# Attention pipeline: transposes directly behind the scores, both minima first, and the next pair's evictions put off behind the probabilities

## The chip, the cores and the metric

One NeuronCore of a Trainium2 chip runs the whole program. The metric is device time in microseconds (us), from launch to end, lower is better. The kernel's time before is the median of three runs, 2943.85 us (2941.52 to 2948.66).

## What is computed

Two layers of a backbone over 1024 latent tokens (a grid of 16 rows by 64 columns) with 256 context tokens, model width 1024. The first layer mixes tokens with Fourier transforms and long convolutions, the second with attention; each ends with a gated feed-forward network. The change touches the attention of the second layer alone. It has 16 heads of 64 channels. A query sees a window of 8 rows by 16 columns of latent keys, with a position bias, and all 256 context keys. Queries are taken in chunks of 16 columns, whose windows share 32 key columns:

```python
s_loc = jnp.einsum("bcqhd,bicjhd->bhcqij", q_r, k_b).astype(jnp.float32) * scale + bias[None]
s_loc = jnp.where(col_ok[:, :, None, :], s_loc, -jnp.inf)
s_ctx = jnp.einsum("bcqhd,bjhd->bhcqj", q_r, kc).astype(jnp.float32) * scale
s = jnp.concatenate([s_loc.reshape(B_, H, n_chunk, NA_QCOLS, n_loc), s_ctx], axis=-1)
p = jax.nn.softmax(s, axis=-1).astype(v.dtype)
...
o = (jnp.einsum("bhcqij,bicjhd->bcqhd", p_loc, v_b)
     + jnp.einsum("bhcqj,bjhd->bcqhd", p[..., n_loc:], vc))
...
y_lat = neighbourhood_attention(q, k, v, kc, vc, rpb).reshape(B_, L, D_MODEL) @ w_out
```

## The kernel before, in words

Numbers are carried as a high and a low half (`wh`, `wl` and the like), so a product is three matmuls; "splitting" a result means a ScalarE instruction that rounds it to the high half and then a VectorE instruction that subtracts that half for the low one.

The attention stage works on 64 items: 8 pairs of heads, times 2 halves of the rows (`hf`), times 4 chunks of columns (`c`). An item holds 128 queries of both heads. The steps of an item are:

- `attn_bias`: GpSimd (POOL) loads two bias tiles of 128 x 384.
- `attn_scores`: twelve matmuls write four PSUM banks of the pool `sc`: for each of the two heads a context score of 256 columns (`pctx`) and a local one of 384 (`loc`). VectorE takes the minimum of the (negated) context scores (L2050), then adds the bias and takes the minimum over both (L2051, a custom instruction and its accumulator read); ScalarE takes the exponentials of context (L2053) and local part (L2055). This runs head by head. Then ScalarE casts the context probabilities to float16 (L2060), POOL subtracts for the low half (L2061), and a transposing DMA on SyncE's (SP's) queue turns both (L2062).
- `attn_turn`: TensorE (PE) transposes the local probabilities of both heads into two banks of the pool `tr` (L2073), three transposes each. `attn_turned` splits them: two ScalarE copies (L2081) and two VectorE subtractions (L2082). From item 52 on, the context probabilities are transposed by PE too (four transposes), and the second head's three come later, in `attn_late`.
- `attn_values`: 30 matmuls multiply probabilities and values. They write into the unused columns of the `pctx` bank of a later item (`free`), so they come after that bank's first exponential. VectorE then divides by the sum (reciprocal L2107, norm L2108). The last score matmuls of the item behind use banks that this norm reads.
- `attn_send`, for every fourth item: four transposes into a `tr` bank (L2119), a split (L2121, L2122), a store by POOL's queue.

Beside an item, PE works on the preparation of the next pair, `attn_prep` (`lin`): keys, context keys and queries, in groups of 24 matmuls that fill a bank of the pool `pq` (for pair 0, which is prepared ahead of the loop, a bank of `sc`). Whatever ends a group is issued at that place: a split of keys (L300, L302), context keys (L1971, L1972) or queries (L1978, L1979), and the splits of value tiles, which DMA brings (`value`: L1955 on POOL, L1956 on ScalarE, L1957 on VectorE). A pair's preparation takes 24 portions, three for each of eight items; `fetch` issues it up to a target. For the items of the last pair `first_part(0)`, the first part of the output projection, takes its place; its weights `w_out2` come by POOL's queue.

In the loop (`attention`) PE, ScalarE, VectorE and POOL run in the order in which the code issues; only SP's order is set by the scheduler. One round issues: the bias of item k+3, the send of k-2, the late transposes of k-1, the scores of k+1 with their whole softmax, a third of the preparation, the transposes of k, a third, the values of k-1, the split of the transposes of k, a third.

Of the kernel before, what the change touches and what calls it, by code (L numbers as in the profile page):

```python
# [10 lines left out]
F32 = mybir.dt.float32  # L11
# [190 lines left out]
class Builder:  # L202
# [1705 lines left out]
    def attn_prep(self, pr, u):  # L1908
# [8 lines left out]
        def lin(wh, wl, pc, view=lambda x: x):  # L1917
            nonlocal step, acc
            yield None
            acc = self.SC() if pr == 0 else self.PQ()  # L1920
            for kb in range(KB):
                for w, part in ((wh, 0), (wh, 1), (wl, 0)):
                    self.mm(acc[:, :WID[pc]], w[:, kb * P:(kb + 1) * P], view(u.ap(part, kb, pc)),
                            kb == 0 and w is wh and part == 0, kb == KB - 1 and w is wl)
                step += 1
                for c in range(5):
                    if step == loads[c]:
                        load(c)
                    if step == turns[c]:
                        value(c)  # L1930
                yield WID[pc] / 1024

        def by_chunk(x):
            return x.rearrange("p (r h c) -> p h r c", r=8, h=4)

# [27 lines left out]
        for pc in (0, 1, 2):  # L1963
            if pc == 1:
                wq = self.halves_of("wq", pr)
            yield from lin(*wk, pc)
            w = WID[pc]
            if pc < 2:
                self.split(acc, *(t[:, pc * 512:pc * 512 + w] for t in (kh, kl)))
            else:  # L1970
                nc.scalar.mul(kc[:, :w], acc[:, :w], -1.0)  # L1971
                nc.vector.scalar_tensor_tensor(kc[:, w:], acc[:, :w], -1.0, kc[:, :w].bitcast(F32), op0=MUL, op1=SUB)  # L1972
        for pc in (0, 1):
            if pc == 1 and pr < 7:
                self.aw = self.halves_of("wk", pr + 1)
            yield from lin(*wq, pc, by_chunk)
            qh, ql = self.S2(F32R), self.S2(F32R)
            nc.scalar.mul(qh, acc, self.qinv)  # L1978
            nc.vector.scalar_tensor_tensor(ql, acc, self.qinv, qh.bitcast(F32), op0=MUL, op1=SUB)  # L1979
            qs[pc] = (qh, ql)  # L1980
# [3 lines left out]
    def attention(self, u, fill):  # L1984
        self.prep, self.osb, self.aw = {}, {}, None
        self.od = [[self.DR([P, LAT], F16) for _ in range(2)] for _ in range(8)]
        self.accumulators(pq=2, sc=4, tr=2)
# [14 lines left out]

        for k in range(2):
            piece(self.attn_bias, k)
        e = mybir.EngineType
        with self.tc.manual_schedule(engines={e.PE, e.Activation, e.DVE, e.Pool}):
            for k in range(-1, 65):
                piece(self.attn_bias, k + 3)
                piece(self.attn_send, k - 2)
                piece(self.attn_late, k - 1)  # L2010
                piece(self.attn_scores, k + 1)
                fetch((k * 3 + 8) * n / 24)
                piece(self.attn_turn, k)
                fetch((k * 3 + 9) * n / 24)
                free = state[k + 1]["free"] if k + 1 < 64 else self.SC()[:, 256:]
                if 0 <= k - 1 < 64:
                    self.attn_values(state[k - 1], *items[k - 1], free)
                piece(self.attn_turned, k)
                fetch((k * 3 + 10) * n / 24)
            piece(self.attn_send, 63)  # L2020
# [12 lines left out]
    def attn_scores(self, s, pr, hf, c):  # L2033
# [3 lines left out]
        bias = s["bias"]  # L2037
# [3 lines left out]
        for acc, keys, w in ((pctx, kc, 256), (loc, kw, 384)):  # L2041
            for x, y in ((0, 0), (0, 1), (1, 0)):
                for hd in (0, 1):
                    r = slice(hd * 64, hd * 64 + 64)
                    self.mm(acc[hd][:, :w], qc[x][r], keys[y][r], x == 0 and y == 0, x == 1)
        st = self.pt.tile([P, 16], F32, tag="st", name=self.nm("st"))
        cm, mx, s["rv"] = (st[:, 2 * i:2 * i + 2] for i in range(3))
        pc = self.T()
        for i in (0, 1):
            nc.vector.tensor_reduce(cm[:, i:i + 1], pctx[i][:, :256], axis=AX, op=MIN)  # L2050
            nc.vector.tensor_tensor_reduce(bias[i], loc[i][:, :384], bias[i], -1.0, cm[:, i:i + 1], ADD, MIN,  # L2051
                                           mx[:, i:i + 1])
            nc.scalar.activation(pc[:, i * 256:i * 256 + 256], pctx[i][:, :256], AF.Exp, bias=mx[:, i:i + 1],  # L2053
                                 scale=-1.0)
            nc.scalar.activation(bias[i], bias[i], AF.Exp, bias=mx[:, i:i + 1], scale=-1.0)  # L2055
        s["pts"], s["free"] = [None] * 3, pctx[0][:, 256:]
# [10 lines left out]
    def attn_turn(self, s, *item):  # L2067

        s["ps"] = []
        for k, src, n in s["ways"][:2]:  # L2070
# [3 lines left out]
            s["ps"].append((k, ps, n * P))  # L2074
        del s["ways"][:2]

    def attn_turned(self, s, *item):

        for k, ps, w in s["ps"]:
            t = s["pts"][k] = self.S2(F16, 1024)  # L2080
            self.nc.scalar.copy(t[:, :w], ps[:, :w])  # L2081
            self.nc.vector.tensor_tensor(t[:, 512:512 + w], ps[:, :w], t[:, :w], SUB)  # L2082

    def attn_late(self, s, *item):

        if s["ways"]:
            self.attn_turn(s)
            self.attn_turned(s)
# [53 lines left out]
    def run(self):  # L2142
# [391 lines left out]
```

## Time and profile before

| what | value |
|---|---|
| median of the runs | 2943.85 us |
| the profiled execution's own time | 2943.7 us |
| its span, first to last instruction | 2941.8 us |
| mean granted TensorE clock | 0.979 |
| busy share: TensorE, VectorE, ScalarE, GpSimd | 94%, 71%, 55%, 20% |
| first score matmul of the loop | at 1802.49 us |
| last score matmuls of the loop's last item begin | at 2230.35 us |

All profile lines come from this one execution, on core 0. In a line of the timeline stand the start in us, the duration, the engine, the source line, the operation, output <- inputs, shapes, how many alike, and in brackets the time the engine had sat idle and what ended that. In a line of the waits stand who waited, for whom, the total in us, how often, and the longest. Names such as `sc`, `tr`, `pq` are PSUM banks, `wh` and `wl` weights, `s`, `t`, `g`, `tk` tiles in SBUF, `st` the minima and sums. Ends of matmuls are modelled, so a row's duration is longer than the distance to the next matmul, and idle time of PE is seen too short.

### The profile page before, as it was taken

The page shows a single profiled execution, that of the slowest core. Times are in us where ns is not written, and L with a number is a line of the kernel's source. Part 1 is how long each engine was busy: PE and PEld are TensorE (multiplying, and loading weights), DVE is VectorE, ACT ScalarE, POOL GpSimd, SP SyncE. Part 2 cuts the span into 40 slices and gives each one's busy share as a digit, 9 for nine tenths or more (in the row PEclk, how much of TensorE's full clock was granted, in tenths as well). Part 3 has the DMA queues.
Part 4 walks back from the last instruction along what each step waited for, and adds up shares of the span by engine and source line. Part 5 has one row for each costly group of instructions (what it writes and reads, how often), then busy time and mean ns, then how long its engine had stood idle before and what let it go on. Part 6 is the DMA issues. An engine that isn't in the chain of part 4 may idle for free. (4 is left out here: it accounts for less than half of the span.)

```text
span 2941.8 us, 46325 instructions
## 1 busy us (share of the span) xinstructions
PE 2765.3 (94%) x16419; PEld 1689.4 (57%) x16419; DVE 2078.4 (71%) x3857; ACT 1622.9 (55%) x2857; POOL 602.8 (20%) x993
## 2 busy tenths in 40 slices
PE   6989999899989999999999998999989999999998
PEld 3766557888879544444556744565655444444555
DVE  4778777675557898886886765666665778765755
ACT  4674325454665676655564554566553467564543
POOL 1012013354121121122120112333332022112000
PEclk8999999999999999999999999999999999999999
DMA  7574435359595665557994996766655566424753
GB/s 257 188 270 171 150 116 172 112 177 330 219 357 181 212 219 199 195 197 271 336 311 133 339 351 196 155 150 145 163 159 170 202 238 238 162 94 173 238 191 125
DMA packets 322083, 607.60 MB, mean 207 GB/s; under 512 B 89910, under 2 KB 129528, under 8 KB 321850
## 3 DMA queue, kind: packets, MB, share of 16 engines
q1 hardware_dynamic: 252378, 384.38, 40.0%
q0 software_dynamic: 67168, 216.06, 21.0%
q10 hardware_dynamic: 2304, 4.20, 0.4%
q8 instruction: 129, 2.11, 0.3%
q14 instruction: 104, 0.85, 0.1%
HBM read 455.33 MB, written 135.53 MB: 201 GB/s over the span
## 5 line engine op out<-in xcount | busy, mean ns | idle before, releaser
L1462 PE MATMUL ps<-s,s 128*128 128x512 f16 x2244 | 506.3, 381 | 10.2 <-ACT g L1467 6.0
L1462 PEld LDWEIGHTS <-s 128*128 128x128 f16 x2640 | 257.9, 98 | 328.7 <-issue 22.0
L296 PE MATMUL ps<-s,wh 128*128 128x256 f32 (+3 forms) x1764 | 399.3, 330 | 11.5 <-ACT wh L300 5.4
L1231 ACT ACTIVATE s<-s,c 128x512 f16<-128x512 f32 (+1 forms) x324 | 234.3, 753 | 150.8 <-DMA s<-d 85.6
L1232 DVE SCALAR_TENSOR_TENSOR s<-s,c,s 128x512 f16<-128x512 f32 (+1 forms) x324 | 247.6, 793 | 89.0 <-ACT s L1231 88.7
L1679 PE MATMUL ps<-s 128*128 128x512 f16 (+2 forms) x1308 | 303.6, 378 | 2.0 <-DVE s L1232 2.0
L296 PE MATMUL ps<-s,wl 128*128 128x256 f32 (+3 forms) x882 | 263.4, 331 | 3.3 <-DMA wl<-d 2.0
L296 PE MATMUL pq<-s,wh 128*128 128x512 f16 (+1 forms) x908 | 252.1, 354 | 5.9 <-DMA wh<-d 4.0
L1679 PEld LDWEIGHTS <-s 128*128 128x128 f16 x1536 | 148.4, 98 | 179.0 <-issue 6.8
L296 PEld LDWEIGHTS <-wh 128*128 128x128 f16 x1664 | 153.6, 99 | 163.0 <-issue 33.7
L287 POOL DMA_DIRECT2D d<-s x201 | 109.1, 543 | 648.9 <-DVE s L1523 186.0
L348 ACT CAST mat<-cs 128x1024 fp32r<-128x1024 f16 (+2 forms) x120 | 111.3, 935 | 139.4 <-PE ps L296 52.6
L296 PEld LDWEIGHTS ps<-s,wh 128*128 128x128 f32 x1088 | 177.3, 192 | 18.1 <-ACT wh L300 5.7
L296 PE MATMUL ps<-s,mat 128*128 128x512 f32 x696 | 182.0, 408 | 3.5 <-DVE s L302 3.2
L1462 PE MATMUL ps<-s,wh 128*128 128x512 f16 x608 | 182.2, 379 | 1.7 <-DVE g L1476 1.3
L296 PE MATMUL sc<-s,s 128*128 128x65 f16 (+3 forms) x2688 | 154.7, 234 | 16.5 <-DVE s L2108 10.0
L296 PEld LDWEIGHTS <-s 128*128 128x128 f16 x2400 | 114.4, 98 | 79.9 <-issue 12.4
L296 PE MATMUL pq<-s,wl 128*128 128x512 f16 (+1 forms) x454 | 157.9, 354 | 0.0
L296 PEld LDWEIGHTS ps<-s,mat 128*128 128x128 f32 x696 | 134.5, 195 | 37.7 <-DVE s L302 4.0
L1264 ACT ACTIVATE t<-s 128x1024 bf16<-128x1024 f32 (+1 forms) x164 | 141.5, 864 | 14.9 <-DVE c L483 9.4
L2053 ACT ACTIVATE t<-sc,st 128x256 f32<-128x256 f32 x128 | 60.7, 474 | 144.3 <-DVE st L2051 138.5
L296 PEld LDWEIGHTS <-wl 128*128 128x128 f16 x832 | 82.0, 99 | 83.2 <-DMA wl<-d 3.8
(445 smaller groups left out, 5603.3 us busy)
## 6 DMA issues: line engine op xcount, KB each, us to landing
s<-d SPq DMA_DIRECT2D x294, 256.0 KB, 4.4
d<-s POOLq DMA_DIRECT2D x157, 256.0 KB, 3.6
s<-in_down SPq DMA_DIRECT2D x154, 256.0 KB, 4.9
s<-in_ada_w POOLq DMA_DIRECT2D x48, 512.0 KB, 4.9
s<-in_gate SPq DMA_DIRECT2D x46, 512.0 KB, 4.0
s<-in_up SPq DMA_DIRECT2D x46, 512.0 KB, 4.2
d<-g POOLq DMA_DIRECT2D x87, 256.0 KB, 3.3
d<-tk POOLq DMA_DIRECT2D x82, 256.0 KB, 4.3
```

The source lines that it names most:

```text
L287: self.last_ldr = self.nc.gpsimd.dma_start(out, in_).ins
L296: return self.nc.tensor.matmul(o, l, r, start=st, stop=sp).ins
L348: self.nc.scalar.copy(m, st)
L1231: nc.scalar.activation(hi, src, AF.Copy, scale=scale)
L1232: nc.vector.scalar_tensor_tensor(lo, src, scale, hi, op0=MUL, op1=SUB)
L1264: self.nc.scalar.activation(junk[:, :t.shape[1]], t, AF.Abs, scale=2.0 ** -15, accum_out=st[:, k:k + 1])
L1462: nc.tensor.matmul(ps, x[:, sl], y, start=first and j == 0 and x is wh and y is xh, stop=j == 3 and x is wl, skip_group_check=True)
L1679: m = nc.tensor.matmul(acc[j][:, c0:c1], x[:, sl], y[:, xs], start=first and k == 0, stop=last and k == 2, skip_group_check=True)
L2053: nc.scalar.activation(pc[:, i * 256:i * 256 + 256], pctx[i][:, :256], AF.Exp, bias=mx[:, i:i + 1], scale=-1.0)
```

## The change

It has five parts.

1. The round is issued anew: send of k-2, scores of k+1 (matmuls only), transposes of k directly behind them, then the softmax of k+1, half of the preparation, the values of k-1, the late transposes of k with their split, half of the preparation.
2. The softmax (now `attn_softmax`) takes both heads' minima of the context first, then both heads' minima with bias and the exponentials. The split of the transposes (`turned`) is woven in: its ScalarE copies ahead of the first exponential, its VectorE subtractions behind the second minimum with bias.
3. What a group of the preparation ends with (splits of keys, context keys, queries and values) is collected in `self.later` and issued at the next `flush`: one stands behind the softmax, one behind the late transposes. For pair 0 it is issued at once, as before.
4. Pair 0's preparation uses the pool `pq`, and the pools are set up in the order `sc`, `tr`, `pq`.
5. The weights `w_out2` of the first part of the output projection are loaded by SP's queue instead of POOL's.

```diff
-            acc = self.SC() if pr == 0 else self.PQ()
+            acc = self.PQ()
...
                     if step == turns[c]:
-                        value(c)
+                        later(lambda c=c: value(c))
...
+        def later(work):
+            if pr == 0:
+                work()
+            else:
+                self.later.append(work)
...
-        self.accumulators(pq=2, sc=4, tr=2)
+        self.accumulators(sc=4, tr=2, pq=2)
...
+        def flush():
+            while self.later:
+                self.later.pop(0)()
...
                 piece(self.attn_send, k - 2)
-                piece(self.attn_late, k - 1)
                 piece(self.attn_scores, k + 1)
-                fetch((k * 3 + 8) * n / 24)
                 piece(self.attn_turn, k)
-                fetch((k * 3 + 9) * n / 24)
+                piece(self.attn_softmax, k + 1)
+                flush()
+                fetch((k * 3 + 8.5) * n / 24)
                 free = state[k + 1]["free"] if k + 1 < 64 else self.SC()[:, 256:]
                 if 0 <= k - 1 < 64:
                     self.attn_values(state[k - 1], *items[k - 1], free)
-                piece(self.attn_turned, k)
+                piece(self.attn_late, k)
+                flush()
                 fetch((k * 3 + 10) * n / 24)
+            flush()
...
         for i in (0, 1):
             nc.vector.tensor_reduce(cm[:, i:i + 1], pctx[i][:, :256], axis=AX, op=MIN)
+        for i in (0, 1):
             nc.vector.tensor_tensor_reduce(bias[i], loc[i][:, :384], bias[i], -1.0, cm[:, i:i + 1], ADD, MIN,
                                            mx[:, i:i + 1])
+            if i == 0:
+                self.turned(0)
             nc.scalar.activation(pc[:, i * 256:i * 256 + 256], pctx[i][:, :256], AF.Exp, bias=mx[:, i:i + 1],
                                  scale=-1.0)
             nc.scalar.activation(bias[i], bias[i], AF.Exp, bias=mx[:, i:i + 1], scale=-1.0)
+        self.turned(1)
...
-    def attn_turned(self, s, *item):
-
-        for k, ps, w in s["ps"]:
-            t = s["pts"][k] = self.S2(F16, 1024)
-            self.nc.scalar.copy(t[:, :w], ps[:, :w])
-            self.nc.vector.tensor_tensor(t[:, 512:512 + w], ps[:, :w], t[:, :w], SUB)
+    def turned(self, part):
+
+        for pts, k, ps, w in self.turns:
+            if part == 0:
+                t = pts[k] = self.S2(F16, 1024)
+                self.nc.scalar.copy(t[:, :w], ps[:, :w])
+            else:
+                t = pts[k]
+                self.nc.vector.tensor_tensor(t[:, 512:512 + w], ps[:, :w], t[:, :w], SUB)
+        if part:
+            self.turns = []
...
-                    (self.ld if pc else self.ldr)(x[:, :768], self.halves[("w_out2", nb)][:, k * 1024:k * 1024 + 768])
+                    self.ld(x[:, :768], self.halves[("w_out2", nb)][:, k * 1024:k * 1024 + 768])
```

The change moves what each engine does in a row. On VectorE, one item (one whose number modulo 8 is 2) stood so before: minimum and minimum with bias by head, a key split of the preparation (L302), the reciprocal and norm of the values, the subtractions from the `tr` banks, a value split (L1957).

```order
L2050 TENSOR_REDUCE st_19672<-sc_19658 128x1
L2051 ISA g_19429,st_19672<-sc_19656,g_19429,st_19672 128x384
L2051 ISA st_19672 128x1
L2050 TENSOR_REDUCE st_19672<-sc_19659 128x1
L2051 ISA s_4132_19431,st_19672<-sc_19657,s_4132_19431,st_19672 128x384
L2051 ISA st_19672 128x1
L302 TENSOR_TENSOR s_4112_19314<-pq_19481,s_4111_19313 128x512
L2107 RECIPROCAL st_19449<-sc_19658 128x2
L2108 TENSOR_TENSOR s_4181_19713<-sc_19658,st_19449 128x128
L2082 TENSOR_TENSOR s_4182_19746<-tr_19696,s_4182_19746 128x384
L2082 TENSOR_TENSOR s_4183_19749<-tr_19700,s_4183_19749 128x384
L1957 SCALAR_TENSOR_TENSOR s_4184_19755<-t_19488,c_17518,s_4184_19755 128x512
```

The same item on VectorE now (L2072, L2074 are the minima, L2110 the subtractions, L1975 the value split, L2138 and L2139 reciprocal and norm):

```order
L2072 TENSOR_REDUCE st_19676<-sc_19654 128x1
L2072 TENSOR_REDUCE st_19676<-sc_19655 128x1
L2074 ISA g_19429,st_19676<-sc_19652,g_19429,st_19676 128x384
L2074 ISA st_19676 128x1
L2074 ISA s_4132_19431,st_19676<-sc_19653,s_4132_19431,st_19676 128x384
L2074 ISA st_19676 128x1
L2110 TENSOR_TENSOR s_4177_19681<-tr_19668,s_4177_19681 128x384
L2110 TENSOR_TENSOR s_4178_19683<-tr_19672,s_4178_19683 128x384
L1975 SCALAR_TENSOR_TENSOR s_4181_19697<-t_19418,c_17518,s_4181_19697 128x512
L2138 RECIPROCAL st_19457<-sc_19654 128x2
L2139 TENSOR_TENSOR s_4183_19711<-sc_19654,st_19457 128x128
```

The subtractions moved ahead of the norm, the value split from behind the norm to ahead of it, and the key split to behind it. On ScalarE the same item had, before, exponentials, the cast L2060, the key split L300, the copies L2081 and the value split:

```order
L2053 ACTIVATE t_19673<-sc_19658,st_19672 128x256
L2055 ACTIVATE g_19429<-g_19429,st_19672 128x384
L2053 ACTIVATE t_19673<-sc_19659,st_19672 128x256
L2055 ACTIVATE s_4132_19431<-s_4132_19431,st_19672 128x384
L2060 CAST s_4176_19682<-t_19673 128x512
L300 CAST s_4111_19313<-pq_19481 128x512
L2081 CAST s_4182_19746<-tr_19696 128x384
L2081 CAST s_4183_19749<-tr_19700 128x384
L1956 ACTIVATE s_4184_19755<-t_19488,c_17518 128x8x64
```

On ScalarE now (L2107 the copies, L2078 and L2080 the exponentials, L2086 the cast, L1974 the value split):

```order
L2107 CAST s_4177_19681<-tr_19668 128x384
L2107 CAST s_4178_19683<-tr_19672 128x384
L2078 ACTIVATE t_19677<-sc_19654,st_19676 128x256
L2080 ACTIVATE g_19429<-g_19429,st_19676 128x384
L2078 ACTIVATE t_19677<-sc_19655,st_19676 128x256
L2080 ACTIVATE s_4132_19431<-s_4132_19431,st_19676 128x384
L2086 CAST s_4179_19692<-t_19677 128x512
L1974 ACTIVATE s_4181_19697<-t_19418,c_17518 128x8x64
L300 CAST s_4109_19309<-pq_19485 128x512
```

The copies moved from behind the cast to ahead of the first exponential. On PE the transposes stood behind the first third of the preparation (`pq` rows):

```order
L296 LDWEIGHTS wh_19104
L296 MATMUL pq_19689<-s_3554_16624,wh_19104 128x256
L296 LDWEIGHTS wl_19105
L296 MATMUL pq_19689<-s_3554_16624,wl_19105 128x256
L2073 MATMUL tr_19696<-c_86,g_19328 128x128 x3
L2073 MATMUL tr_19700<-c_86,s_4117_19330 128x128 x3
L296 LDWEIGHTS wh_19104
L296 MATMUL pq_19689<-s_3568_16677,wh_19104 128x256
```

Now, in the same item, they stand directly behind the last score matmuls (`sc` rows, 128x384):

```order
L296 MATMUL sc_19652<-s_3965_18449,s_4090_19158 128x384
L296 MATMUL sc_19653<-s_3965_18449,s_4090_19158 128x384
L2098 MATMUL tr_19668<-c_86,g_19324 128x128 x3
L2098 MATMUL tr_19672<-c_86,s_4115_19326 128x128 x3
L296 LDWEIGHTS wh_19100
L296 MATMUL pq_19701<-s_3554_16624,wh_19100 128x256
```

So the transposes come six preparation matmuls earlier here, and the preparation of a round is cut in two instead of three.

More of the change, by code (lines that the diff above doesn't have):

```diff
@@ L1934, in by_chunk, with key, context_key, query @@
             return x.rearrange("p (r h c) -> p h r c", r=8, h=4)
+        def later(work):
[3 more added lines that the diff above has]
+                self.later.append(work)
+        def key(acc, cols):
+            self.split(acc, kh[:, cols], kl[:, cols])
+        def context_key(acc):
+            nc.scalar.mul(kc[:, :256], acc[:, :256], -1.0)
+            nc.vector.scalar_tensor_tensor(kc[:, 256:], acc[:, :256], -1.0, kc[:, :256].bitcast(F32), op0=MUL, op1=SUB)
+        def query(acc, pc):
+            qh, ql = qs[pc] = self.S2(F32R), self.S2(F32R)
+            nc.scalar.mul(qh, acc, self.qinv)
+            nc.vector.scalar_tensor_tensor(ql, acc, self.qinv, qh.bitcast(F32), op0=MUL, op1=SUB)
         def load(c):
@@ L1966, in attn_prep @@
             yield from lin(*wk, pc)
[L1967 to L1972, printed above, removed]
+            later((lambda acc=acc: context_key(acc)) if pc == 2 else
+                  (lambda acc=acc, pc=pc: key(acc, slice(pc * 512, pc * 512 + 512))))
         for pc in (0, 1):
@@ L1976, in attn_prep @@
             yield from lin(*wq, pc, by_chunk)
[L1977 to L1980, printed above, removed]
+            later(lambda acc=acc, pc=pc: query(acc, pc))
         self.prep[pr] = (qs, (kh, kl), (kc[:, :256], kc[:, 256:]), vt)
@@ L1984, in attention @@
     def attention(self, u, fill):
-        self.prep, self.osb, self.aw = {}, {}, None
+        self.prep, self.osb, self.aw, self.later, self.turns = {}, {}, None, [], []
         self.od = [[self.DR([P, LAT], F16) for _ in range(2)] for _ in range(8)]
-        self.accumulators(pq=2, sc=4, tr=2)
+        self.accumulators(sc=4, tr=2, pq=2)
         n = sum(x or 0 for x in self.attn_prep(0, u))
@@ L2036, in attn_scores @@
         qs, kk, kc, _ = self.prep[pr]
-        bias = s["bias"]
         loc, pctx = ([self.SC(), self.SC()] for _ in range(2))
@@ L2045, in attn_scores, with attn_softmax @@
                     self.mm(acc[hd][:, :w], qc[x][r], keys[y][r], x == 0 and y == 0, x == 1)
+        s["pctx"], s["loc"], s["free"] = pctx, loc, pctx[0][:, 256:]
+    def attn_softmax(self, s, pr, hf, c):
+        nc = self.nc
+        pctx, loc, bias = s["pctx"], s["loc"], s["bias"]
         st = self.pt.tile([P, 16], F32, tag="st", name=self.nm("st"))
@@ L2055, in attn_scores @@
             nc.scalar.activation(bias[i], bias[i], AF.Exp, bias=mx[:, i:i + 1], scale=-1.0)
-        s["pts"], s["free"] = [None] * 3, pctx[0][:, 256:]
+        self.turned(1)
+        s["pts"] = [None] * 3
         s["ways"] = [(1, bias[0], 3), (2, bias[1], 3)]
@@ L2067, in attn_turn @@
     def attn_turn(self, s, *item):
-        s["ps"] = []
         for k, src, n in s["ways"][:2]:
@@ L2073, in attn_turn @@
                 self.nc.tensor.transpose(ps[:, j * P:(j + 1) * P], src[:, j * P:(j + 1) * P], self.ident)
-            s["ps"].append((k, ps, n * P))
+            self.turns.append((s["pts"], k, ps, n * P))
         del s["ways"][:2]
-    def attn_turned(self, s, *item):
-        for k, ps, w in s["ps"]:
-            t = s["pts"][k] = self.S2(F16, 1024)
-            self.nc.scalar.copy(t[:, :w], ps[:, :w])
-            self.nc.vector.tensor_tensor(t[:, 512:512 + w], ps[:, :w], t[:, :w], SUB)
+    def turned(self, part):
[8 more added lines that the diff above has]
+            self.turns = []
     def attn_late(self, s, *item):
@@ L2087, in attn_late @@
             self.attn_turn(s)
-            self.attn_turned(s)
+        self.turned(0)
+        self.turned(1)
     def attn_values(self, s, pr, hf, c, o):
```

## The prediction

> **What bounds the kernel now.** I read the page first, then the windows, the waits and the timeline of the attention stage, the only stage whose compute order the change touches. TensorE (PE) is the bound: it is busy 94% of the span.
>
> ```profile
> PE 2765.3 (94%) x16419; PEld 1689.4 (57%) x16419; DVE 2078.4 (71%) x3857; ACT 1622.9 (55%) x2857; POOL 602.8 (20%) x993
> ```
>
> So a gain is a PE wait that goes. The windows (us, then busy time of each engine with its instructions, last but two the granted PE clock) split the stage into 51 steady items (one item is one pair of heads, one half, one chunk), ten late ones, and the end of the loop; three of its stretches ran at half clock.
>
> ```profile
> 1817.33:2156.64 339.31, 309.13 (x3269) 204.74 (x3269) 220.74 (x588) 205.49 (x435) 120.50 (x202) 0.99 0.66 151
> 2156.64:2230.35 73.71, 62.24 (x633) 41.28 (x632) 47.05 (x122) 35.98 (x77) 21.32 (x40) 0.93 0.47 154
> 2230.35:2245.48 15.13, 14.45 (x160) 9.31 (x160) 7.92 (x20) 5.31 (x11) 3.72 (x7) 1.00 0.36 114
> ...
> 1771.20:1781.40 10.20, 4.58 (x11) 1.68 (x12) 8.79 (x19) 5.09 (x9) 4.39 (x14) 0.50 1.04 401
> ...
> 2170.50:2177.30 6.80, 6.10 (x37) 4.55 (x38) 3.63 (x10) 2.99 (x7) 0.73 (x2) 0.50 0.15 52
> 2197.80:2201.20 3.40, 3.40 (x36) 2.04 (x35) 1.08 (x4) 0.00 (x0) 0.85 (x2) 0.50 0.90 293
> ```
>
> PE's waits in the steady items, then in the late ones:
>
> ```profile
> PE tr L2119 <- DVE s L2082: 15.1, 12, 1.7
> PE sc L296 <- DVE s L2108: 10.0, 13, 1.0
> PE sc L296 <- ACT t L2053: 4.2, 7, 0.8
> ```
>
> ```profile
> PE tr L2073 <- DVE s L2082: 5.9, 5, 2.7
> PE pq L296 <- DMA wh<-d: 4.0, 2, 2.3
> PE tr L2119 <- DVE s L2082: 1.1, 2, 0.9
> ```
>
> Three kinds: transposes wait until VectorE (DVE) has read their bank (L2082); the eighth score matmul waits for the norm L2108, which reads the bank it writes; and in the late items weights come late. The steady items repeat every eight (the preparation of the next pair fills eight items). One cycle, from score start to score start:
>
> ```profile
> 1916.43 0.39 PE L296 MATMUL sc<-s,s 64*128 64x256 f32 x2
> ...
> 1969.70 0.39 PE L296 MATMUL sc<-s,s 64*128 64x256 f32 x2
> ```
>
> That is 53.27 us, 6.37 times in the 339.31. The timeline shows one item with its send before it and the next item behind it (S, the start of the scores, is 1951.72):
>
> ```profile
> 1951.16 0.63 PE L2119 MATMUL tr<-c,s 128*128 128x128 f32 x4 [0.81 <-DVE s L2082]
> ...
> 1951.72 1.16 PE L296 MATMUL sc<-s,s 64*128 64x256 f32 x12
> ...
> 1951.82 0.59 ACT L2121 CAST tk<-tr 128x512 f16<-128x512 f32 x1 [1.08 <-PE tr L2119]
> ...
> 1953.05 0.41 DVE L2050 TENSOR_REDUCE st<-sc 128x1 f32<-128x256 f32 x1
> ...
> 1953.60 0.62 DVE L2051 CUSTOM_DVE_ANT_0 g<-sc,g,st 128x384 f32<-128x384 f32 x1
> ...
> 1954.26 0.47 ACT L2053 ACTIVATE t<-sc,st 128x256 f32<-128x256 f32 x1 [1.85 <-DVE st L2051]
> ...
> 1954.63 0.60 ACT L2055 ACTIVATE g<-g,st 128x384 f32<-128x384 f32 x1
> ...
> 1955.68 0.59 PE L296 MATMUL pq<-s,wh 128*128 128x512 f16 x2
> ...
> 1955.72 0.60 ACT L2055 ACTIVATE s<-s,st 128x384 f32<-128x384 f32 x1
> ...
> 1956.23 0.60 ACT L2060 CAST s<-t 128x512 f16<-128x512 f32 x1
> ...
> 1956.33 0.59 PE L296 MATMUL pq<-s,wh 128*128 128x512 f16 x2
> ...
> 1956.73 0.69 ACT L1978 ACTIVATE s<-pq,c 128x512 fp32r<-128x512 f32 x1
> ...
> 1957.07 0.62 PE L296 MATMUL sc<-s,s 64*128 64x256 f32 x6
> ...
> 1957.46 0.75 DVE L1979 SCALAR_TENSOR_TENSOR s<-pq,c,s 128x512 fp32r<-128x512 f32 x1 [2.14 <-ACT s L1978]
> ...
> 1958.32 0.29 DVE L2108 TENSOR_TENSOR s<-sc,st 128x128 f32<-128x128 f32 x1
> ...
> 1958.76 0.77 PE L296 MATMUL sc<-s,s 64*128 64x384 f32 x5 [0.89 <-DVE s L2108]
> ```
>
> See two things. First, PE's own work: three preparation matmuls take 0.65 (1955.68 to 1956.33), 0.2155 each. This item (1951.72 to 1957.07) has 12 such matmuls, no PE idle and 5.35 us, so scores, transposes and values are 5.35 - 12 x 0.2155 = 2.76. A cycle holds 108 preparation matmuls of 512 columns' worth and two sends of 0.56 (1951.72 - 1951.16): 8 x 2.76 + 108 x 0.2155 + 1.12 = 46.5 us. So 6.8 of 53.27 are lost; the waits named sum to only 29.3 / 6.37 = 4.6, because matmul ends are modelled. Second, the chain that ends at 1958.76: exponentials, the cast L2060, an eviction pair (L1978, L1979) that stands ahead of the norm, the norm, PE.
>
> **The change, part by part.**
>
> *Preparation of pair 0 in pq banks.* PE sat idle before it, for a copy of a bank; its first weight load had come long before, and the copy of the pq bank was long done:
>
> ```profile
> 1768.60 0.56 ACT L1893 COPY tk<-pq 128x512 f32<-128x512 f32 x1
> ...
> 1771.70 0.10 PEld L296 LDWEIGHTS <-wh 128*128 128x128 f16 x1 [3.15 <-DMA wh<-d]
> ...
> 1776.82 1.01 PE L296 MATMUL sc<-s,wh 128*128 128x512 f16 x2 [7.77 <-ACT t L1893]
> ...
> 1804.29 0.80 PE L296 MATMUL sc<-s,s 64*128 64x384 f32 x5 [1.00 <-DVE s L1979]
> ```
>
> Now the weights decide: 1776.82 - 1771.70 = 5.1 earlier. The 1.00 at item 0 (its fourth score bank was still being evicted) goes too. Of half clock: 11 matmuls took 4.58 in the window against 11 x 0.2155 = 2.37; with 7.77 - 5.1 = 2.7 idle left instead of 7.77 I take 0.9 back of 2.2 (bounds 0 and 2.2). Together -7.0, bounds -5 and -8.4. The Trainium skill ("TensorE: Matmul & The Clock Gate", Part 1: The HAM clock gate) says that the clock halves after at least one idle window of about 3.4 us and comes back after a busy one; by it 2.7 us of idle would not halve it, and this part would be -8.3. The trace speaks against it: the half clock from 2170.50 lies round the late items' longest wait, 2.7 us, and no wait there is longer.
>
> *Steady items.* Transposes directly behind the scores, the copies ahead of the exponentials and the subtractions ahead of the norm free the tr banks early: the 15.1 us go. What is late next is the norm, since it still stands behind the deferred eviction, and the copies now precede the exponentials. Worked from S: transposes at 1.16 (the scores' length), first copy 0.55 later (an estimate from the send: copy 0.66 behind four transposes, three here), two copies of 0.37 each (an estimate from their 0.485 busy, pitch as for exponentials), first exponential 2.45. Then 0.37 + 0.51 twice gives the cast at 4.24, the eviction's ScalarE half at 4.74 (0.50). Query halves: DVE 0.73 later (1956.73 to 1957.46), the norm 0.86 behind it, PE 0.44 behind that: S + 6.77. Value halves:
>
> ```profile
> 1921.78 0.72 ACT L1956 ACTIVATE s<-t,c 128x512 f16<-128x512 f32 x1
> ...
> 1921.96 1.15 POOL L2061 TENSOR_TENSOR s<-t,s 128x512 f16<-128x512 f32 x1 [4.15 <-ACT s L2060]
> ...
> 1922.54 1.12 DVE L1957 SCALAR_TENSOR_TENSOR s<-t,c,s 128x512 f16<-128x512 f32 x1 [2.17 <-ACT s L1956]
> ...
> 1924.91 0.74 DVE L1957 SCALAR_TENSOR_TENSOR s<-t,c,s 128x512 f16<-128x512 f32 x1
> ```
>
> Their DVE half starts 0.76 later, and is 1.12 long beside the POOL subtraction of the cast instead of 0.74; the order now always puts them right behind that cast. The norm is then 0.86 + 1.12 - 0.75 = 1.23 behind: PE at 4.74 + 0.76 + 1.23 + 0.44 = S + 7.2. In the items behind a send the first minimum starts at S + 1.33 (1953.05), the exponential 0.42 + 0.55 + 0.66 later, so all is 0.45 later.
>
> PE reaches the next item's eighth score matmul 0.40 after its own work (at 1958.76 - 0.89 the seventh had ended, 0.80 behind S; an end lags the next start by 0.4, an estimate from 0.59 for two at 0.2155). Own work is 5.35 with 12 preparation matmuls, 6.0 with 15, 5.4 with 24 of half width. By position in the cycle (item number modulo 8), own work, norm at PE, wait: 2 (behind a send): 5.4, 7.6, 1.8; 3: 6.0, 7.2, 0.8; 4: 5.35, 7.2, 1.4; 5 (query and a value split of half size, a query's chain and some 0.4 more, then a send, which needs the norm at 6.0): 7.2, 1.2; 7 (query): 6.0, 6.8, 0.4; 6 (behind a send, nothing deferred): 0.3 for the exponential, whose bank the values are written in; 0 and 1: nothing ahead of the norm, 0. Sum 5.9: the cycle is 52.4, and (52.4 - 53.27) x 6.37 = -5.5. A wait shifts its whole item, so it isn't handed on. Bounds: each of six waits 0.4 shorter (value splits at 0.74): -15 more, so -20; each 0.5 longer (copies or the deferral later than I set them): +19, so +14. I take the middle, since its chain is that of the rows.
>
> *Late items (score matrices of three transposes).* The third transposes stand behind the values, when their bank has long been subtracted: of 7.0 us I take 6.4. Weights of the output projection leave POOL's queue for SP's, which in these items has no transposing DMA left. On POOL they stood behind a send's store and what that waits for:
>
> ```profile
> 2193.43 0.55 POOL L287 DMA_DIRECT2D d<-tk x1 [3.93 <-DVE tk L2122]
> ```
>
> I take all of the 4.0. SP's later loads move with it; I cost that at nothing, covered by the matmuls behind the stage, 3 us if not. The two half clocks cost (6.10 + 3.40) / 2 = 4.75; with those waits gone I take half, 2.5. -12.9, bounds -9 and -17. *The end of the loop* (15.13): its last transposes, too, stand behind scores or values: -1, bounds 0 and -2.
>
> **The sum** is made against the profiled execution's 2943.7, which is the median of the runs, 2943.85, within 0.2: 2943.7 - 7.0 - 5.5 - 12.9 - 1.0 = **2917.3**.
>
> **Rivals.**
> *Waits halve.* If the copies squeeze in before the exponentials for nothing and the value splits escape POOL, 3.0 of the cycle's loss remain: 49.5, -24, 2899; with none left, 46.5 and 2880. For it: most named waits are on L2082, which goes. Against: the norm's chain above. Chance 0.18.
> *The ring eats it.* Copies ahead of the exponentials push every norm 0.2 to 0.4 later than I set: the cycle is 53.3 to 54.3, and only the head, the late and the last items gain, 2923 to 2929. Chance 0.16.
> *Slower.* Each of the six later by nearly 1 us: cast, deferred eviction, norm and PE become one ring without slack, as the eviction waits for ScalarE, which waits for the transposes, which wait for the last norm. From S + 8.1 for the norm at PE it decides: 5.7 more a cycle, 58.1, +31 against -21, 2954. For it: the row at 1958.76 is such a ring already. Against: items 0, 1 and 6 have nothing ahead of the norm. Chance 0.06.
> *Head and tail don't come* (weights stand as late on SP, the pq bank isn't free): -5.5 alone, 2938. Chance 0.07.
> *The clock never falls* in the head and the late items, since no PE idle is left that is long enough: 1.3 + 2.3 more, 2914, inside my forecast's span; chance 0.1, part of the forecast's. The clock gate of the Trainium skill's page would give that.
>
> **How the numbers follow.** My forecast, 2908 to 2925, has 0.53. About what a measurement can tell from no change is 0.3%, 8.8 us: faster lies below 2935. Faster 0.53 + 0.18 + 0.14 and a little of the rest: 0.86; within 0.3%: 0.08; slower: 0.06. The range takes in the forecast, the eaten ring and most of the halved waits: 2892 to 2939.
>
> **Right or wrong.** Right: a first preparation matmul near 1771.7; no wait of the send on the subtraction at position 1; norm waits of 0.4 to 1.8 in positions 2, 3, 4, 7; cycle 52.4; late items near 61. Wrong: a cycle under 50 or over 53.3, the first matmul still behind a copy, weights still waited for.

## The result and the profile after

The changed kernel takes 2921.72 us (median of 4 runs, 2916.52 to 2925.08), the kernel before 2945.62 (4 runs, 2941.52 to 2948.66). The ratio is 0.9918 with a 95% interval of 0.9895 to 0.9941: 24 us faster. The forecast was 2917.3, in a range of 2892 to 2939. The profiled execution took 2916.52, its span is 2914.8.

Its windows for the head, the steady items (2 to 52) and the late items (53 to 62), to be laid beside those of before:

```profile
1771.20:1781.40 10.20, 9.09 (x29) 3.57 (x30) 9.17 (x21) 5.68 (x10) 4.38 (x14) 0.67 1.04 406
1812.15:2139.96 327.81, 309.84 (x3269) 205.31 (x3268) 220.85 (x586) 201.26 (x434) 120.61 (x202) 1.00 0.66 158
2139.96:2199.16 59.20, 57.11 (x632) 39.59 (x632) 45.19 (x123) 35.71 (x76) 15.00 (x29) 1.00 0.53 177
```

The steady items went from 339.31 to 327.81, the late ones from 73.71 to 59.20, and there the clock is full now. In the head PE waits for its weights and no longer for a copy:

```profile
1772.31 1.04 PE L296 MATMUL pq<-s,wh 128*128 128x512 f16 x2 [3.00 <-DMA wh<-d]
```

One cycle of eight items, from score start to score start:

```profile
1908.60 0.62 PE L296 MATMUL sc<-s,s 64*128 64x256 f32 x6
...
1960.04 0.80 PE L296 MATMUL sc<-s,s 64*128 64x256 f32 x8
```

That is 51.44 us, where it was 53.27 and PE's own work is 46.5. PE's waits in the steady items, then in the late ones (L2139 is the norm, L2150 the send's transposes, L2078 the first exponentials):

```profile
PE sc L296 <- DVE s L2139: 12.8, 20, 0.9
PE tr L2150 <- DVE s L2139: 3.5, 6, 0.6
PE sc L296 <- ACT t L2078: 1.7, 7, 0.3
```

```profile
PE sc L296 <- ACT t L2078: 1.6, 4, 0.4
PE sc L296 <- DVE s L2139: 0.4, 1, 0.4
```

In these items no wait is left for a subtraction from a `tr` bank, nor for weights. All that is left in the steady items hangs on the norm or on an exponential. The timeline of the item at position 2 and the start of the next shows the chain that sets it:

```profile
1915.07 1.16 PE L296 MATMUL sc<-s,s 64*128 64x256 f32 x12
...
1916.40 0.74 DVE L2072 TENSOR_REDUCE st<-sc 128x1 f32<-128x256 f32 x2
...
1917.78 0.47 ACT L2078 ACTIVATE t<-sc,st 128x256 f32<-128x256 f32 x1 [0.17 <-DVE st L2074]
...
1919.52 0.61 ACT L2086 CAST s<-t 128x512 f16<-128x512 f32 x1
...
1920.03 0.72 ACT L1974 ACTIVATE s<-t,c 128x512 f16<-128x512 f32 x1
...
1920.21 1.15 POOL L2087 TENSOR_TENSOR s<-t,s 128x512 f16<-128x512 f32 x1 [2.89 <-ACT s L2086]
...
1920.78 1.13 DVE L1975 SCALAR_TENSOR_TENSOR s<-t,c,s 128x512 f16<-128x512 f32 x1 [1.63 <-ACT s L1974]
1920.93 0.79 PE L296 MATMUL sc<-s,s 64*128 64x256 f32 x7
...
1922.02 0.29 DVE L2139 TENSOR_TENSOR s<-sc,st 128x128 f32<-128x128 f32 x1
...
1922.46 0.77 PE L296 MATMUL sc<-s,s 64*128 64x384 f32 x5 [0.74 <-DVE s L2139]
```

From S = 1915.07: exponential at 2.71, cast 4.45, value split on ScalarE 4.96 and on VectorE 5.71 (1.13 long beside POOL), norm 6.95, PE 7.39. The eighth score matmul of the next item stood ready and waited.

Counted by stages of the loop, in us (a start is that of the scores):

| stage | before | after | change | forecast |
|---|---|---|---|---|
| last matmul ahead of pair 0's preparation, to its first | 8.16 | 3.38 | -4.8 | -5.1 |
| that first matmul to the first score | 25.67 | 26.40 | +0.7 | -0.9 |
| items 0 and 1 | 14.84 | 13.44 | -1.4 | -1.0 |
| items 2 to 52 | 339.3 | 327.8 | -11.5 | -5.5 |
| items 53 to 62 | 73.7 | 59.2 | -14.5 | -12.9 |
| item 63 to the last value matmul | 14.9 | 15.1 | +0.2 | -1.0 |
| from there to the end | 696.6 | 700.5 | +3.9 | 0 |

### The profile page after: what moved, and what is told of

Read it like the earlier page. It is cut to its first block, busy times and chain, and to the rows that moved or that the text cites. A ratio compares the mean times of both kernels' runs of the same rounds, so it can differ in the third digit from the quotient of the medians.

```text
span 2914.8 us, 46336 instructions
## 1 busy us (share of the span) xinstructions
PE 2761.7 (95%) x16419; PEld 1686.2 (58%) x16419; DVE 2078.8 (71%) x3857; ACT 1619.3 (56%) x2857; POOL 593.3 (20%) x977
## 5 line engine op out<-in xcount | busy, mean ns | idle before, releaser
L296 PE MATMUL pq<-s,wh 128*128 128x512 f16 (+1 forms) x988 | 273.6, 355 | 5.0 <-DMA wh<-d 3.0
L296 PEld LDWEIGHTS <-wh 128*128 128x128 f16 x1664 | 159.6, 99 | 152.6 <-issue 13.6
L296 PE MATMUL pq<-s,wl 128*128 128x512 f16 (+1 forms) x494 | 172.3, 354 | 0.0
L296 PEld LDWEIGHTS <-s 128*128 128x128 f16 x2400 | 113.2, 98 | 80.0 <-issue 11.5
L2107 ACT CAST s<-tr 128x384 f16<-128x384 f32 (+1 forms) x140 | 62.9, 490 | 137.2 <-PE tr L2098 136.9
```

Source lines behind the costliest of these rows:

```text
L296: return self.nc.tensor.matmul(o, l, r, start=st, stop=sp).ins
```

## The experiments

Totals of different kernels carry a spread that has nothing to do with attention: ahead of it, where no edit touches the code, the profiled executions differ by over 12 us (the last matmul ahead of pair 0's preparation starts between 1768.6 and 1781.2). So the stage that an edit touches is read from the trace, and the totals stand beside it.

### The deferral ahead of the norm: taken away, and all deferral taken away

The first kernel drops the flush ahead of the norm; everything deferred is issued behind the norm and the late transposes.

```diff
                 piece(self.attn_softmax, k + 1)
-                flush()
                 fetch((k * 3 + 8.5) * n / 24)
```

> The changed kernel without the flush ahead of the norm: all deferred evictions stand behind the norm and the late transposes. Changed kernel: a cycle of eight items 51.44, PE waits for the norm 16.3 in the steady items. Theory (the deferred eviction ahead of the norm makes the norm late): waits for the norm under 4, cycle 48 to 50.5, total 6 to 22 us under the changed kernel. Rival (the wait moves on: evictions behind the norm push the next minima and exponentials, and PE waits for these): waits for exponentials over 10, cycle 51 to 53, total within 10 us either way.

Measured: a cycle of 47.4 to 47.6, the steady items 302.2 instead of 327.8, median 2892.47 (2887.32 to 2893.85), ratio to the kernel before 0.9817 (0.9799 to 0.9835). PE's waits in the steady items, all of them:

```profile
PE sc L296 <- ACT t L2077: 2.0, 8, 0.3
```

The norm is waited for no more. This kernel's timeline shows where the value split went; here the norm is L2138, the minimum L2071:

```profile
1925.69 0.29 DVE L2138 TENSOR_TENSOR s<-sc,st 128x128 f32<-128x128 f32 x1
...
1926.61 1.16 PE L296 MATMUL sc<-s,s 64*128 64x256 f32 x12
1926.65 1.13 DVE L1975 SCALAR_TENSOR_TENSOR s<-t,c,s 128x512 f16<-128x512 f32 x1 [0.67 <-ACT s L1974]
...
1927.71 0.74 DVE L2071 TENSOR_REDUCE st<-sc 128x1 f32<-128x256 f32 x2
```

The split runs beside the next scores, delays the minima to 1.1 behind their start, and PE loses nothing by it. It is as slow as before: of the groups by line, value splits of 512 columns in the changed kernel and here (count, busy us, mean ns):

```profile
L1975 DVE SCALAR_TENSOR_TENSOR s<-t,c,s 128x512 f16<-128x512 f32 x28 | 31.6, 1128 | 45.9 <-ACT s L1974 41.8 <-DMA s<-s 4.0
```

```profile
L1975 DVE SCALAR_TENSOR_TENSOR s<-t,c,s 128x512 f16<-128x512 f32 x28 | 31.3, 1117 | 21.5 <-ACT s L1974 18.1 <-DMA s<-s 2.0 <-DMA t<-d 1.3
```

So the split's length beside POOL costs PE nothing where it stands behind the norm; what costs is its place ahead of the norm. The theory holds in its direction, and its rival (the wait moves on) falls. The size is beyond the theory: I expected a cycle of 48 to 50.5 and 6 to 22 us, and it is 47.4 and 29.

The second kernel issues each eviction where its group of the preparation ends.

```diff
         def later(work):
-            if pr == 0:
+            if True:
                 work()
```

> The changed kernel without deferral: each eviction is issued where its group of the preparation ends. Theory (what counts is how much stands ahead of the norm; undeferred it is a key, a context key, a key and a value split instead of four value and two query splits): waits for the norm 8 to 13 in the steady items, cycle 50 to 51.3, total 1 to 9 us under the changed kernel. Rival (an eviction at its own place makes VectorE and ScalarE wait for PE's group and holds up the norm behind it, so deferral is what brings the gain): cycle 52.3 to 54, total 5 to 16 us over.

Measured: cycle 49.33, steady items 314.8, median 2907.56 (2902.32 to 2909.24), ratio 0.9868 (0.9849 to 0.9887). Its waits in the steady items:

```profile
PE tr L2150 <- DVE s L2139: 3.6, 6, 0.6
PE sc L296 <- DVE s L2139: 3.5, 13, 0.4
PE sc L296 <- ACT t L2078: 2.3, 7, 1.0
```

The direction is the theory's, the size beyond it: I expected 8 to 13 us of norm waits, a cycle of 50 or more and 1 to 9 us less than the changed kernel; the norm waits come to 7.1, and it takes 14 us less. So deferral to the place ahead of the norm, as the change has it, costs 2.1 us a cycle against none at all.

### The old order, with evictions behind the norm

In the kernel before, the evictions are collected as in the change and issued at the end of the round; nothing else is changed.

```diff
                 piece(self.attn_turned, k)
+                while self.later:
+                    self.later.pop(0)()
                 fetch((k * 3 + 10) * n / 24)
```

> The kernel before, with one thing changed: the evictions and value splits of the preparation are put off and issued at the end of the round, behind the norm and the subtractions; order of matmuls and transposes, minima, head and weights' queue as before. Before: cycle 53.27, median near 2946. Theory (in both kernels it is the eviction ahead of the norm that costs; the norm early, the subtractions behind it come early too): cycle 47.5 to 49.5, waits for the norm under 2, the sends' waits on the subtraction under 6, total 24 to 40 us under the kernel before. Rival (without early transposes the tr banks bind as before): the waits on the subtractions stay over 12, cycle 51 to 53.3, total 0 to 15 us under.

Measured: cycle 49.4, steady items 314.0 against 339.3, median 2913.23 (2912.30 to 2920.26), ratio 0.9887 (0.9870 to 0.9903). Its waits in the steady items (L2134 the send's transposes, L2097 the subtractions):

```profile
PE pq L296 <- DVE s L302: 10.2, 7, 1.7
PE tr L2134 <- DVE s L2097: 6.1, 12, 0.8
```

The norm waits are gone and the send's wait on the subtractions fell from 15.1 to 6.1, though the transposes stand where they stood. A new wait came that neither theory named: a key split put off holds its `pq` bank until PE wants it again. In the steady items alone this one edit gains 25 us, the whole change 11.5.

These three kernels, the kernel before and the changed one can be read together: the order of transposes, minima and copies on one side, the place of the evictions on the other. Time of the steady items, and a cycle, in us:

| order | each eviction at its own place | put off to behind the norm | put off to ahead of the norm |
|---|---|---|---|
| as before | 339.3, 53.3 | 314.0, about 49.4 | not tried |
| as changed | 314.8, 49.3 | 302.2, 47.4 | 327.8, 51.4 |

So the new order alone gains 24.5 us, and evictions behind the norm alone gain 25.3; both together gain 37, not the sum. (In each of these, 1.6 us are a half clock that the kernel before alone had in the steady items.) The change has the new order, and its flush ahead of the norm takes 13 of the 24.5 back.

### The transposes on PE

The changed kernel, with the transposes back behind the first half of the preparation on PE; VectorE's and ScalarE's order stays.

```diff
-                piece(self.attn_turn, k)
-                piece(self.attn_softmax, k + 1)
-                flush()
+                held, self.later = self.later, []
                 fetch((k * 3 + 8.5) * n / 24)
+                held, self.later = self.later, held
+                piece(self.attn_turn, k)
+                piece(self.attn_softmax, k + 1)
+                flush()
+                self.later.extend(held)
```

> The changed kernel with one part undone on TensorE alone: the transposes stand behind the first half of the preparation, while VectorE and ScalarE keep the changed order (copies ahead of the exponentials, evictions as deferred). Theory (transposes, copies and exponentials are one chain): the first exponential comes 1.3 to 1.9 us later in every item, values wait for it 1.1 us in every item, cycle 58 to 62, total 40 to 70 us over the changed kernel. Rival (the early transposes matter only for the tr banks, and the preparation covers the rest): cycle 52 to 54, total 4 to 16 us over.

Measured: cycle 60.46, median 2984.49 (2983.59 to 2992.29), ratio 1.0124 (1.0107 to 1.0141): slower than the kernel before. Its waits in the steady items:

```profile
PE sc L296 <- ACT t L2081: 51.5, 51, 1.7
PE sc L296 <- DVE s L2142: 15.0, 20, 1.1
PE tr L2153 <- DVE s L2142: 4.7, 6, 0.8
```

Every one of the 51 items waits for its first exponential (here L2081), as it stands behind copies that wait for the transposes. With copies ahead of the exponentials the early transposes are a condition. How much of the 24.5 us of the new order is theirs and how much the copies', no run separates.

### The minima, and the copies

The changed kernel, with minimum and minimum with bias by head again:

```diff
             nc.vector.tensor_reduce(cm[:, i:i + 1], pctx[i][:, :256], axis=AX, op=MIN)
-        for i in (0, 1):
             nc.vector.tensor_tensor_reduce(bias[i], loc[i][:, :384], bias[i], -1.0, cm[:, i:i + 1], ADD, MIN,
```

> The changed kernel with one part undone: minimum and minimum with bias by head again, everything else as changed. Theory (the copies from the tr banks, not the minima, set the first exponential): cycle 51.4 to 51.9, total within 4 us of the changed kernel. Rival (both minima first shorten VectorE's part of the ring): cycle over 52.4, total 6 us or more over.

Measured: cycle 51.53 against 51.44, median 2918.98 (2917.36 to 2919.80), ratio 0.9893 (0.9878 to 0.9907), which the changed kernel's interval overlaps. The theory holds: this part of the change is worth 0.1 us a cycle (0.6 in the steady items, 328.45 against 327.81), and nothing that the totals show.

Without the flush ahead of the norm, and with the copies between the two heads' exponentials:

```diff
-            if i == 0:
-                self.turned(0)
             nc.scalar.activation(pc[:, i * 256:i * 256 + 256], pctx[i][:, :256], AF.Exp, bias=mx[:, i:i + 1],
                                  scale=-1.0)
             nc.scalar.activation(bias[i], bias[i], AF.Exp, bias=mx[:, i:i + 1], scale=-1.0)
+            if i == 0:
+                self.turned(0)
```

> No flush ahead of the norm, and the copies from the tr banks moved from ahead of the first head's exponentials to between the two heads' exponentials. Without the flush ahead of the norm alone: cycle 47.4 to 47.6, waits for exponentials 3.8 in all, median 2892.5. Theory (the last steady wait is that of the values for the first exponential, behind two copies): waits for exponentials under 1, cycle 46.5 to 47.1, total 2 to 6 us less. Rival (the copies come later, and with them the subtractions and the second exponential, so the wait moves to the norm): cycle 47.4 or more, total the same or more.

Measured: cycle 49.6 instead of 47.4, median 2910.64 (2909.10 to 2917.74), ratio 0.9870 (0.9855 to 0.9884). My theory failed here. The timeline, from one item into the next (L2106 copies, L2109 subtractions, L2138 norm, L2071 minima, L2075 first exponential):

```profile
1922.18 0.85 ACT L2106 CAST s<-tr 128x384 f16<-128x384 f32 x2
...
1922.68 1.02 DVE L2109 TENSOR_TENSOR s<-tr,s 128x384 f16<-128x384 f32 x2 [0.94 <-ACT s L2106]
...
1923.87 0.29 DVE L2138 TENSOR_TENSOR s<-sc,st 128x128 f32<-128x128 f32 x1
...
1925.07 1.14 DVE L1975 SCALAR_TENSOR_TENSOR s<-t,c,s 128x512 f16<-128x512 f32 x1 [0.91 <-ACT s L1974]
...
1926.74 0.74 DVE L2071 TENSOR_REDUCE st<-sc 128x1 f32<-128x256 f32 x2
...
1928.04 0.47 ACT L2075 ACTIVATE t<-sc,st 128x256 f32<-128x256 f32 x1 [2.53 <-DVE st L2073]
1928.57 1.06 PE L296 MATMUL sc<-s,s 128*128 128x65 f16 x30 [0.25 <-ACT t L2075]
```

The later copies push the subtractions, the norm, the evictions behind it and so the next minima; ScalarE then sits idle 2.53 for them, and PE waits for the exponential all the same. The rival had the direction, but named the norm as the new wait, and over the whole loop PE waits most for the exponential, and not once for the norm:

```profile
PE sc L296 <- ACT t L2075: 10.6, 29, 0.6
```

The ring runs through VectorE.

### Weights and head

The changed kernel, with the output projection's weights on POOL's queue again:

```diff
-                    self.ld(x[:, :768], self.halves[("w_out2", nb)][:, k * 1024:k * 1024 + 768])
+                    (self.ld if pc else self.ldr)(x[:, :768], self.halves[("w_out2", nb)][:, k * 1024:k * 1024 + 768])
```

> The changed kernel with one part undone: the output projection's weights (first part) come by GpSimd's queue again. Changed kernel: late items (53 to 62) 59.2 us, no wait there for weights. Theory (on GpSimd's queue the weights stand behind a send's store): waits for weights of 3 to 5 us come back, late items 62 to 64, total 2 to 5 us over the changed kernel. Rival (the weights were late only because the late transposes held GpSimd's queue up, through the send): late items stay under 60.5 and the total within 1 us.

Measured: late items 61.5 instead of 59.2, median 2925.53 (2917.78 to 2932.43), ratio 0.9932 (0.9907 to 0.9956). Waits for weights in the late items:

```profile
PE pq L296 <- DMA wh<-d: 1.7, 2, 0.9
```

It lies between the two: the queue is worth 2.3 us, not 3 or more. The rest of the 4.0 went with the other edits of the round; which of them wasn't tried.

The changed kernel, with pair 0 in score banks and the old order of the pools:

```diff
-            acc = self.PQ()
+            acc = self.SC() if pr == 0 else self.PQ()
...
-        self.accumulators(sc=4, tr=2, pq=2)
+        self.accumulators(pq=2, sc=4, tr=2)
```

> The changed kernel with one part undone: pair 0 is prepared in the score banks again, and the pools are set up in the old order. Changed kernel: first preparation matmul at 1772.3, first score matmul at 1798.7, items 0 and 1 together 13.4. Theory (PE waited for a bank's copy, the fourth score bank for an eviction): first matmul near 1776.8, first score near 1802.5, items 0 and 1 together near 14.4, total 4 to 5.5 us over the changed kernel. Rival (the head lies beside DMA that sets the pace of items 0 and 1 anyway): first score later, but the start of item 8 within 1 us of the changed kernel's, total the same.

Measured: its timeline (the part before attention ran 12 us later in this execution, so the waits tell it, not the starts):

```profile
1789.21 1.01 PE L296 MATMUL sc<-s,wh 128*128 128x512 f16 x2 [7.77 <-ACT t L1893]
...
1816.40 0.80 PE L296 MATMUL sc<-s,s 64*128 64x384 f32 x5 [1.33 <-DVE s L1952]
```

Both waits are back. From the last matmul ahead of it to the first score it takes 33.2 instead of 29.8, items 0 and 1 take 15.2 instead of 13.4, together 5.2; the steady and late items are unchanged (327.9, 59.2). Median 2931.96 (2929.12 to 2936.11), ratio 0.9950 (0.9932 to 0.9968). The theory holds in the trace. The medians differ by 10.2, where I had set 4 to 5.5; in the profiled executions 12.1 us more lie ahead of the attention stage and 2.2 behind it, and no run gives a cause for these.

Last, on top of the kernel without the flush ahead of the norm, matmuls that fill PE's wait in the head:

```diff
             acc = self.PQ()
+            if pr == 0 and not pc and not step:
+                for _ in range(14):
+                    self.mm(acc, u.ap(0, 7, 1)[:, :P], u.ap(0, 7, 1), True, True)
```

> No flush ahead of the norm, and 14 extra matmuls of 512 columns (3.0 us, results overwritten) on TensorE where it waits for the first weights of pair 0's preparation; they change nothing in the outputs. Without them TensorE is idle 2.7 us there and the preparation of pair 0 takes 25.1 us, at half clock for its first part. Theory (the idle time before it is what halves the clock): no half clock in the head, preparation 23.0 to 23.6, the loop's first score matmul 1.3 to 2 us earlier counted from the last matmul before the wait. Rival (half clock there has another cause, such as the weight of work before): the preparation stays at 24.6 or more.

Measured: the preparation takes 23.4, with the clock full from the extra matmuls to the first score; median 2894.53 (2888.33 to 2903.92), ratio 0.9813 (0.9790 to 0.9836), no different from without. From the last matmul ahead of PE's wait to the first score it takes 27.0 instead of 28.2, a gain of 1.2 where the theory had at least 1.3. The window of the extra matmuls and the preparation:

```profile
1781.70:1808.17 26.47, 26.45 (x134) 13.02 (x133) 16.47 (x31) 10.90 (x19) 5.72 (x16) 1.00 0.84 304
```

The full clock fits the theory but doesn't show it, for another kernel, the one with late transposes, idles 2.7 us there and keeps the full clock without such matmuls:

```profile
1777.90:1801.30 23.40, 23.40 (x120) 11.65 (x120) 13.85 (x27) 10.23 (x18) 4.90 (x14) 1.00 0.85 299
```

### A version that beats both

The kernel without the flush ahead of the norm already does. With more of the preparation ahead of the values:

```diff
-                fetch((k * 3 + 8.5) * n / 24)
+                fetch((k * 3 + 9) * n / 24)
```

> No flush ahead of the norm, and two thirds of the round's preparation (instead of a half) between the transposes and the values. Without the latter: cycle 47.4 to 47.6, 2892.5. Theory (the values still wait for the first exponential in two positions of eight, and more work ahead of them covers that): no such wait in the steady items, cycle 46.8 to 47.3, 0 to 5 us less. Rival (values later make the norm later, and the evictions behind it push the next minima): cycle 47.6 to 49, 0 to 8 us more.

Measured: cycle 47.0, steady items 299.1 (302.2 without), median 2889.30 (2888.13 to 2895.22), ratio 0.9802 (0.9788 to 0.9817). The cycle is where the theory put it, and the steady items have no named wait of PE left; the totals of the two overlap. It is the fastest measured: 0.5 us a cycle above PE's own work.

## Why the prediction was right

**The whole.** The sum was -26.4, the profiled execution gave -27.2 (2943.7 to 2916.5), and the medians -23.9. The sum is better than its terms: two were too small by 7.6 together, three too large by 6.6. That it falls so near is luck.

**Steady items** (-5.5 forecast, -11.5 measured). The mechanism was right: waits on the subtractions went, and the norm behind a deferred eviction took their place, which the kernel without the flush ahead of the norm shows. The size was off by 1.0 in 5.9. What the working did not price by themselves are the two halves of the change, which pull against each other here: without deferral the new order takes the cycle to 49.3, and the deferred evictions ahead of the norm bring it back to 51.4. Of the 11.5, moreover, 1.6 is the clock's. I counted three stretches at half clock, and there was a fourth, inside the steady items of the kernel before, where an item took 6.98 and its like 5.38; the changed kernel has none there:

```profile
1979.40:1982.80 3.40, 3.40 (x19) 2.55 (x16) 2.44 (x7) 1.64 (x4) 0.55 (x1) 0.50 0.68 207
```

Time above PE's own work by position in the cycle, a wait counted in the item in which it falls:

| position | 1 | 2 | 3 | 4 | 5 | 6 | 7 | 0 | sum |
|---|---|---|---|---|---|---|---|---|---|
| forecast | 0 | 0 | 1.8 | 0.8 | 2.6 | 0.3 | 0 | 0.4 | 5.9 |
| measured | -0.1 | 0.5 | 1.2 | 0.7 | 2.1 | 0.2 | 0.0 | 0.3 | 4.9 |

At position 2 I set the norm at PE to S + 7.6 and it came at 7.39: the second minimum starts 0.33 behind the first, where I took 0.42, the minimum with bias 0.33 behind that (at 1917.06), where I took 0.55, and the exponential comes 2.71 behind S, where I had 2.9. (My own terms, 1.33, 0.42, 0.55 and 0.66, add up to 2.96, so the delay behind a send is 0.51 and not 0.45; and the cast's terms give 4.21, not 4.24.) There, too, the item behind a send waits for its exponential, which I had given to position 6 alone, and what PE lost there it could not lose again to the norm. Position 5, with the send, was 0.5 too dear. "A wait shifts its whole item, so it isn't handed on" held.

**Late items** (-12.9, -14.5). I took half of the half clock's 4.75 back; the window shows clock 1.00, so all of it went. That term was short by 2.3. The waits on banks and weights went as said, though the weights' queue has only 2.3 of the 4.0.

**Head** (-7.0, -5.5). PE's start and the fourth score bank were as worked, 4.8 and 1.4. The clock was not: I took 0.9 back, and it cost 0.7 more, as 14 of the first steps were slow where 11 had been.

**The end of the loop** (-1.0, +0.2): wrong. I took its transposes' waits away, 0.7 in all before; a wait of the same kind is still there, and longer:

```profile
PE tr L2098 <- DVE s L2110: 1.1, 1, 1.1
```

**Behind the loop** I took nothing, with 3 us if SP's loads were not covered. It was 3.9, and 3.2 of it falls at one place where PE waits for no load. Where the feed-forward network begins, the scheduler put one matmul of a `pq` group ahead of twelve others; in the changed kernel it waits with all of them behind it, where before they had run first. Before, then after:

```profile
2335.58 2.75 PE L1462 MATMUL ps<-s,s 128*128 128x512 f16 x12
2338.66 0.38 PE L1462 MATMUL pq<-s,s 128*128 128x512 f16 x1 [0.33 <-ACT s L1358]
```

```profile
2307.81 0.59 PE L1462 MATMUL pq<-s,s 128*128 128x512 f16 x1 [2.68 <-ACT s L1358]
2308.20 4.27 PE L1462 MATMUL ps<-s,s 128*128 128x512 f16 x13
```

The clock (last but two) is lower there, too, before and then after:

```profile
2334.40:2342.60 8.20, 7.19 (x34) 3.09 (x32) 8.20 (x14) 4.51 (x9) 0.00 (x0) 1.00 0.19 68
```

```profile
2303.50:2313.40 9.90, 7.22 (x27) 2.75 (x26) 9.90 (x16) 6.75 (x13) 0.00 (x0) 0.80 0.10 37
```

Matmul by matmul (both kernels run the same 16419, counted from the last), the changed kernel is 30.84 us ahead when this place begins and 27.63 behind it. The kernel without the flush ahead of the norm has the old order there and loses nothing at it. It is as long behind the loop (701.5) as it loses 2.1 and 2.6 elsewhere, around two stretches at half clock:

```profile
2219.90:2223.30 3.40, 3.40 (x10) 1.21 (x8) 0.00 (x0) 0.00 (x0) 0.00 (x0) 0.50 0.01 4
2329.10:2335.90 6.80, 5.98 (x15) 2.13 (x15) 6.76 (x13) 6.80 (x21) 2.23 (x5) 0.50 0.48 172
```

What brings the order and the half clocks on in one kernel and not in another stays open; over all kernels the time behind the loop lies between 695.2 and 705.0.

**The rivals.** "Waits halve" (a cycle of 49.5) didn't come, yet two kernels show how near it lay: the new order without deferral, 49.3, and the old order with evictions behind the norm, 49.4. "Slower" named the right ring; it closes fully where the transposes are late (60.5). "The clock never falls" came in the late items and not in the head.

## What to carry to other kernels

When a bank's reader (here the norm) holds up the tensor engine, ask first what stands ahead of that reader on its queue: moving evictions from ahead of it to behind it was worth as much (25 us on the old order) as the whole reordering of transposes, minima and copies (24.5 without deferral), and both together 37. The same evictions put off to a place ahead of that reader cost 13 us. An eviction put off must still return its bank in time, and work put behind the critical reader delays the head of the next round, so look for the wait that comes next. Work out a wait as the difference of two arrivals, position by position, and check the sum against the loss in a whole cycle, since waits between modelled matmul ends show only part of it.

## What was unexpected of the hardware

- The value split, VectorE with two inputs from SBUF, takes 743 ns alone and 1130 beside POOL's subtraction (28 of the 512-column splits average 1128 in the changed kernel). Splits with one input in a PSUM bank take the same 751 ns beside such a subtraction as alone (L1979 before, L1952 now), and POOL's subtraction takes its 1150 whether a value split runs beside it or not.
- PE idle of 2.7 to 3.0 us ahead of pair 0's preparation was followed by half clock in six kernels (8 to 14 slow steps) and by none in two, the one without deferral (3.0 us) and the one with late transposes (2.7), though the idle time was the same. So the length of the idle time alone doesn't decide it here. In five of the six the first two to four matmuls behind the wait still ran at full speed.
- Two minima of different banks in a row start 0.33 us apart, each 0.41 long. A minimum with bias that reads the minimum just ahead of it started 0.55 behind that one (at 1953.60); with the other head's minimum between them, it starts 0.33 behind the latter.
